# A fused two-block transformer on one core: the gated branches' sum is kept by VectorE instead of GpSimd

## The chip, the core and the metric

The kernel runs on one core of a Trainium2 chip. The core has five engines, each with an instruction queue of its own that it works off in order: TensorE (PE in the profile, its weight loads PEld), VectorE (DVE), ScalarE (ACT), GpSimd (POOL) and SyncE (SP), which here issues the DMA transfers. The metric is the time of one execution on the device in microseconds (us).

## What is computed

Two blocks of two layers each, on 512 tokens of width 1024, in float32. The first block has a recurrent mixer and a sparse-attention mixer, each with a convolutional feed-forward part. The second block, in which the change lies, has in each layer a mixer of four branches, an expert layer and a gated embedding. The mixer, cut to what matters:

```python
h = rms_norm(x, g_mix[i])
o_a = gqa_block_attention(q, k, v)             # branch 0
o_b = bidir_ssd(z, xs, b, c, dt_f, dt_b, ...)  # branch 1
o_c = diff_block_attention(q1, q2, k1, k2, v, lam, rel_bias)   # branch 2, then a norm
o_d = spatial_gating(uv, ...)                  # branch 3
branches = jnp.stack([o_a, o_b, o_c, o_d], axis=2)
gates = jax.nn.sigmoid(h @ w_branch_gate[i]).reshape(b, s, 4, 1024)
merged = jnp.sum(gates * jnp.einsum('bsnc,ncd->bsnd', branches, w_branch[i]), axis=2)
x = x + merged @ w_out[i]
```

## The kernel before, in words

Activations lie with the channels on the 128 partitions: a tile of 128x512 holds 128 channels of all tokens, and eight of them are the whole width (index d or k). A float32 matrix product is made of three float32r products of a high and a low part (lines 439 to 441): the weights come as a stream of 512 KB chunks (wraw), ScalarE copies each to the high part wh (line 237) and VectorE subtracts it to get the low part wl (line 238). This happens for every chunk, all through the kernel.

The mixer computes the branches in the order 3 (spatial gating), 0 (grouped attention), 1 (SSD, a state-space scan in chunks), 2 (differential attention). While a branch runs, the gate and output products of the branch before it are laid between its steps: `fill` takes a step of the generator `gate_merge` after each step of the branch. For each of the eight d, `gate_merge` does this: eight matmul triples give the gate pg; VectorE scales it with the row norm RB (line 1201), ScalarE takes a tanh (line 1202), two triples give the branch's output pb. For the first branch VectorE writes (1 + tanh) * pb to the running sum m (line 1207). For the other three it writes the product to a buffer mu (line 1210), and GpSimd adds mu to m (line 1211). That is 3 x 8 adds per layer, 48 in all. The merge of branch 0 runs beside SSD, that of branch 1 beside differential attention, that of branch 2 at the end, when no branch is left.

After the last merge, `mixer_out` takes m: ScalarE makes the scaled high part xh (line 1259), VectorE the low part xl (line 1260), and TensorE multiplies with w_out. In the same place small loads are brought in: tri into the buffer RB once the last scaled gate has read it (line 2085), from which ScalarE makes cum (line 2086), and pt (line 2080), from which ph is made (line 348). SyncE also loads the experts' weights ahead there (line 1327).

The PSUM buffers of pg and pb come from a pool of three (mm). mg and mu share three buffers.

The names that the steps below need in the SSD branch: delta and dA come from a softplus, a chain of some twenty small VectorE operations (lines 576 to 586, dA in line 1560); conv scales a projection into pad (line 1595), starts a four-tap convolution on ScalarE (line 1597), adds the other taps on VectorE into cv (line 1599), takes a tanh (line 1602) and multiplies (line 1604 to xs, line 1606 to cv); bch and bcl are the high and low part of two such results (lines 348, 349), which lines 1636 to 1638 multiply; M are the decay products (line 1676).

The program is written in the order above, but the order of each engine's queue is made by a scheduler when the program is built, which goes by its own estimate of what each instruction costs. So a change of one instruction's engine can reorder all queues around it.

Of the kernel before, what the change touches and what calls it, by code (L numbers as in the profile page):

```python
# [202 lines left out]
def halves(t):  # L203
    return t.rearrange("p (a b) -> p a b", a=2)


def unwoven(t):
    return t.rearrange("p (b a) -> p a b", a=2)
# [74 lines left out]
class Kern:  # L283
# [904 lines left out]
    def gate_merge(self, l, n, o, tp, first):  # L1188
        nc = self.nc
        for d in range(KD):  # L1190
            key = ("w_branch_gate_2", l, n * D + d * P)
            if key in self.early:
                pg = self.early.pop(key)
            else:
                pg = self.psum()
                specs = [("w_branch_gate_2", l, k * P, n * D + d * P) for k in range(KD)]
                self.dense(pg, specs, self.xh, self.xl, part=(0, 4))
                yield
                self.dense(pg, specs, self.xh, self.xl, part=(4, KD))
            t = tp.tile([P, S], F32, name="mg", bufs=3)  # L1200
            nc.vector.tensor_mul(halves(t), unwoven(pg), halves(self.RB))
            nc.scalar.activation(t, t, AF.Tanh, scale=0.5)
            pb = self.psum()
            self.dense(pb, [("w_branch_2", (l, n), k * P, d * P) for k in range(2)], *o)
            m = self.mg[d // 4][:, d % 4]
            if first:
                nc.vector.scalar_tensor_tensor(halves(m), halves(t), 1.0, unwoven(pb), op0=OP.add, op1=OP.mult)
            else:
                u = tp.tile([P, S], F32, name="mu", tag="mg", bufs=3)
                nc.vector.scalar_tensor_tensor(halves(u), halves(t), 1.0, unwoven(pb), op0=OP.add, op1=OP.mult)  # L1210
                nc.gpsimd.tensor_add(m, m, u)  # L1211
            yield

    def weave(self, a, b, na, nb):
# [961 lines left out]
```

## Time and profile before

| what | us |
|---|---|
| median of 3 runs | 3472.54 |
| lowest and highest of the runs | 3471.07, 3486.43 |
| the profiled execution | 3472.88 |
| its span, first to last instruction | 3471.1 |
| TensorE busy in the span | 3351.6 |
| VectorE busy | 1708.6 |
| ScalarE busy | 1259.8 |
| GpSimd busy | 420.6 |
| the 48 adds of line 1211 on GpSimd | 70.6 |

The views come from one execution, recorded by the hardware's profiler; times inside it are counted from the span's start. The mixer of layer 0 lies at about 1360 to 1820 us, that of layer 1 at 2410 to 2870. A busy time is the time in which an engine had an instruction in flight; the ends of matmuls are modelled, so a share near 100% for TensorE means that its instructions follow each other without a visible gap. A wait is put down to the instruction that released it last.

### The profile page before, as it was taken

What the parts mean: (1) busy time and instruction counts of PE and PEld (TensorE: products, weight loads), DVE (VectorE), ACT (ScalarE), POOL (GpSimd) and SP (SyncE); (2) the same over time, 40 slices, a digit from 0 to 9 for tenths busy, and PEclk for the clock granted to TensorE, in tenths of its full rate; (3) what the DMA queues carried; (4) which work ended last, traced back from release to release, by engine and by line L of the source; (5) the groups of instructions that cost most, each with busy time, mean ns of one, the idle gap of its engine ahead of it and who ended that gap; (6) DMA issues with size and microseconds to landing.
All of it is one profiled execution on the core that took longest, in us unless ns stands there. A gap on an engine that the chain in (4) does not pass through costs nothing.

```text
span 3471.1 us, 42234 instructions
## 1 busy us (share of the span) xinstructions
PE 3351.6 (97%) x16172; PEld 2340.8 (67%) x16172; DVE 1708.6 (49%) x3191; ACT 1259.8 (36%) x2221; POOL 420.6 (12%) x334
## 2 busy tenths in 40 slices
PE   7899999999999999999999999999999999999997
PEld 6788888866588888876887433327876887433325
DVE  7755454477765454776664111016676664111015
ACT  6533233366543234435633100004435644100004
POOL 1111011022021011210012000002210012000002
PEclk9999999999999999999999999999999999999999
DMA  3233333301023323222255999994221255999993
GB/s 126 92 103 129 103 103 108 110 32 37 19 91 103 101 99 114 74 73 67 88 205 210 381 412 419 419 419 144 76 72 62 88 194 198 382 412 419 419 419 124
DMA packets 173491, 629.06 MB, mean 181 GB/s; under 512 B 19557, under 2 KB 20069, under 8 KB 172521
## 3 DMA queue, kind: packets, MB, share of 16 engines
q1 hardware_dynamic: 173288, 626.36, 48.3%
q8 instruction: 127, 2.08, 0.2%
q14 instruction: 76, 0.61, 0.1%
HBM read 618.14 MB, written 8.14 MB: 180 GB/s over the span
## 4 chain that ended last, share of the span: by engine, by line
PE 78%; DVE 10%; DMA 6%; ACT 3%; issue 1%; POOL 1%; DVEq 0%; SPq 0%; ACTq 0%; POOLq 0%
PE mm L439 14%; PE mm L440 14%; PE mm L441 14%; PE mm L1977 10%; PE o L1977 5%; DMA eraw<-in_exw 3%; DVE wl L238 2%; PE o L891 2%; PE t L875 1%; DMA wraw<-in_exw 1%; ACT wh L237 1%; PE mm L1959 1%; PE o L1647 1%; PE o L1786 1%; DMA raw<-in_exw 1%
## 5 line engine op out<-in xcount | busy, mean ns | idle before, releaser
L439 PE MATMUL mm<-xh,wh 128*128 128x512 f32 (+1 forms) x1936 | 750.7, 388 | 11.7 <-DVE mu L1210 5.5
L441 PE MATMUL mm<-xh,wl 128*128 128x512 f32 (+1 forms) x1936 | 744.0, 384 | 2.7 <-DVE wl L238 2.7
L440 PE MATMUL mm<-xl,wh 128*128 128x512 f32 (+1 forms) x1936 | 743.6, 384 | 0.0
L238 DVE TENSOR_TENSOR wl<-wraw,wh 128x1024 fp32r<-128x1024 f32 x366 | 458.2, 1253 | 353.3 <-ACT wh L237 344.1
L237 ACT ACTIVATE wh<-wraw 128x1024 fp32r<-128x1024 f32 x378 | 398.3, 1055 | 521.9 <-PE mm L440 365.1
L439 PEld LDWEIGHTS mm<-xh,wh 128*128 128x128 f32 (+1 forms) x1936 | 368.5, 190 | 79.6 <-issue 9.0
L441 PEld LDWEIGHTS mm<-xh,wl 128*128 128x128 f32 (+1 forms) x1936 | 367.7, 190 | 63.6 <-issue 5.8
L440 PEld LDWEIGHTS mm<-xl,wh 128*128 128x128 f32 (+1 forms) x1936 | 368.6, 190 | 60.1 <-issue 8.2
L1977 PE MATMUL mm<-eraw,xe 128*64 128x512 f32 x1024 | 241.9, 597 | 1.0 <-DMA eraw<-in_exw 1.0
L371 POOL TENSOR_TENSOR sq<-sq,sqt 128x512 f32<-128x512 f32 x63 | 88.3, 1401 | 1240.8 <-ACT sqt L368 1233.6
L1983 DVE TENSOR_TENSOR hid<-sg,mm 128x512 f32<-128x512 f32 x32 | 22.0, 688 | 364.8 <-PE mm L1977 364.8
L1977 PE MATMUL mm<-raw,xe 128*64 128x512 f32 x656 | 161.9, 599 | 1.3 <-DMA raw<-in_exw 1.1
L1977 PEld LDWEIGHTS mm<-eraw,xe 128*64 128x64 f32 x1024 | 70.6, 136 | 134.6 <-issue 116.1
L612 POOL TENSOR_TENSOR fc<-fc,RB 128x512 f32<-128x512 f32 x48 | 84.8, 1766 | 546.7 <-ACT fc L611 546.7
L439 PE MATMUL mm<-gh,wh 128*128 128x512 f32 x384 | 145.5, 379 | 0.0
L440 PE MATMUL mm<-gl,wh 128*128 128x512 f32 x384 | 145.5, 379 | 0.0
L441 PE MATMUL mm<-gh,wl 128*128 128x512 f32 x384 | 145.5, 379 | 0.0
L1977 PE MATMUL o<-eraw,hidT 128*64 128x512 f32 x560 | 137.2, 605 | 3.9 <-DMA eraw<-in_exw 3.0
L1211 POOL TENSOR_TENSOR mg<-mg,mu 128x512 f32<-128x512 f32 x48 | 70.6, 1470 | 556.1 <-DVE mu L1210 510.8
L2031 ACT ACTIVATE yh<-o,af 128x512 fp32r<-128x512 f32 x32 | 22.0, 687 | 299.0 <-PE o L1977 299.0
L1982 ACT ACTIVATE sg<-mm 128x512 f32<-128x512 f32 x32 | 19.1, 597 | 288.8 <-PE mm L1977 288.6
L2032 DVE SCALAR_TENSOR_TENSOR yl<-o,af,yh 128x512 fp32r<-128x512 f32 x32 | 24.0, 751 | 202.9 <-ACT yh L2031 202.8
(522 smaller groups left out, 5623.6 us busy)
## 6 DMA issues: line engine op xcount, KB each, us to landing
eraw<-in_exw SPq DMA_DIRECT2D x396, 512.0 KB, 9.9
wraw<-in_wst SPq DMA_DIRECT2D x378, 512.0 KB, 3.3
raw<-in_exw SPq DMA_DIRECT2D x234, 512.0 KB, 9.9
wraw<-in_exw SPq DMA_DIRECT2D x136, 512.0 KB, 9.9
pbd<-pbs SPq DMA_DIRECT2D x8, 512.0 KB, 4.8
pb<-pbd SPq DMA_DIRECT2D x4, 1024.0 KB, 11.7
tb<-t5d SPq DMA_DIRECT2D x8, 448.0 KB, 3.2
mixt<-in_mix SPq DMA_DIRECT2D x2, 1344.0 KB, 6.4
```

The lines of the kernel that those rows point to most:

```text
L237: kb.nc.scalar.activation(h, raw, AF.Copy)
L238: (kb.nc.gpsimd if self.pool else kb.nc.vector).tensor_sub(l, raw, h.bitcast(F32))
L371: nc.gpsimd.tensor_add(acc, acc, t)
L439: nc.tensor.matmul(out, a, h, start=(k == 0), stop=False)
L440: nc.tensor.matmul(out, a, l, start=False, stop=False)
L441: nc.tensor.matmul(out, b, h, start=False, stop=(k == n - 1))
L612: nc.gpsimd.tensor_mul(c0, c0, self.RB)
L875: nc.tensor.transpose(pt[:, r * P:(r + 1) * P], srcs(i, r), self.ident)
L891: nc.tensor.matmul(o[0][c % 2 * HD:(c % 2 + 1) * HD], lhs(i), pe, start=(c < 2), stop=False)
L1211: nc.gpsimd.tensor_add(m, m, u)
L1647: nc.tensor.matmul(py[hh * HD:(hh + 1) * HD, sl], xd[:, i, q, h * HD:(h + 1) * HD], MS[hh][:, sl], start=(q == 0 and i == 0), stop=(q == 1 ...
L1977: nc.tensor.matmul(ps[e * CAP:(e + 1) * CAP], x[:, k, off + e * CAP:off + (e + 1) * CAP], raw[:, e], start=(k == 0), stop=(k == KD - 1))
```

## The change

Line 1211, the add of mu to the running sum m, is given to VectorE. Nothing else in the source changes, and the same values are computed.

```diff
             else:
                 u = tp.tile([P, S], F32, name="mu", tag="mg", bufs=3)
                 nc.vector.scalar_tensor_tensor(halves(u), halves(t), 1.0, unwoven(pb), op0=OP.add, op1=OP.mult)
-                nc.gpsimd.tensor_add(m, m, u)
+                nc.vector.tensor_add(m, m, u)
             yield
```

The built program differs in all queues from the start of the SSD branch to the output projection, in both layers alike, and nowhere else. On GpSimd the 24 adds per layer are gone and the rest stands as before. On TensorE the same matmuls stand in another order: between line 1552 and line 1562 there are 58 matmuls of projections where there were 42, and of the gate that follows the conv part 1 stands ahead of line 1636 and 2 ahead of line 1637, where 8 and 12 stood. On SyncE some weight loads (line 226) have moved ahead of an expert load (line 1327) or of pt.

VectorE at the start of the SSD branch, in the softplus (names sp_), a piece of the difference:

```order
 L576 TENSOR_SCALAR sp_u<-sp_e 128x32
 L585 TENSOR_SCALAR sp_r<-dx 128x32
-L1201 TENSOR_TENSOR mg<-mm,RB 128x512
+L1211 TENSOR_TENSOR mg<-mg,mu 128x512
 L577 RECIPROCAL sp_u<-sp_u 128x32
+L1201 TENSOR_TENSOR mg<-mm,RB 128x512
+L578 TENSOR_TENSOR sp_z<-sp_e,sp_u 128x32
 L1593 MEMSET pad 128x2
 L1594 MEMSET pad 128x2
-L578 TENSOR_TENSOR sp_z<-sp_e,sp_u 128x32
 L579 TENSOR_TENSOR sp_z_12230<-sp_z 128x32
-L1210 SCALAR_TENSOR_TENSOR mu<-mg,mm 128x512
```

The first add now stands where the next scaled gate stood, and that has moved behind the reciprocal. The second add follows four rows further down, and a second weight split, a fourth step of line 1599 and a second pad (line 1595) now stand ahead of line 1560.

VectorE at the end of the conv part, up to the second bcl, before:

```order
L1201 TENSOR_TENSOR mg<-mm,RB 128x512
L1606 SCALAR_TENSOR_TENSOR cv<-th,cv 128x512
L1594 MEMSET pad 128x2
L1210 SCALAR_TENSOR_TENSOR mu<-mg,mm 128x512
L238 TENSOR_TENSOR wl<-wraw,wh 128x1024
L349 TENSOR_TENSOR bcl_12540<-cv,bch_12539 128x512
```

and now:

```order
L1211 TENSOR_TENSOR mg<-mg,mu 128x512
L1599 SCALAR_TENSOR_TENSOR cv<-pad,cw,cv 128x512
L238 TENSOR_TENSOR wl<-wraw,wh 128x1024
L1606 SCALAR_TENSOR_TENSOR cv<-th,cv 128x512
L1201 TENSOR_TENSOR mg<-mm,RB 128x512
L1593 MEMSET pad 128x2
L349 TENSOR_TENSOR bcl_12540<-cv,bch_12539 128x512
```

The scaled gate and mu stood ahead of the split and of bcl. Now the split comes first, mu comes after bcl, and an add stands ahead of the last step of line 1599.

ScalarE at the tail, around the last xh, before:

```order
L1202 ACTIVATE mg<-mg 128x512
L237 ACTIVATE wh<-wraw 128x1024
L1259 ACTIVATE xh<-mg 128x512
L2086 ACTIVATE cum<-RB 128x128
L348 ACTIVATE ph<-pt 128x1024
L237 ACTIVATE wh<-wraw 128x1024
```

and now:

```order
L1202 ACTIVATE mg<-mg 128x512
L237 ACTIVATE wh<-wraw 128x1024
L2086 ACTIVATE cum<-RB 128x128
L1259 ACTIVATE xh<-mg 128x512
L237 ACTIVATE wh<-wraw 128x1024
L348 ACTIVATE ph<-pt 128x1024
```

The copy cum has passed the last xh, and the next wh has passed ph. On VectorE, in the same place, the last add stands behind mu and the weight split that follows it.

## Rows read from the trace of the kernel before

**Rows 1.** The page's first part: busy us, share of the span, instructions.

```profile
PE 3351.6 (97%) x16172; PEld 2340.8 (67%) x16172; DVE 1708.6 (49%) x3191; ACT 1259.8 (36%) x2221; POOL 420.6 (12%) x334
```

**Rows 2.** Busy windows, layer 0's mixer: us, PE, PEld, DVE, ACT, POOL, clock, DMA.

```profile
1508.00:1558.00 50.00, 46.38 (x220) 38.22 (x218) 43.59 (x99) 19.46 (x28) 6.67 (x4) 1.00 0.26 85
1558.00:1640.00 82.00, 81.40 (x343) 53.71 (x343) 53.81 (x85) 44.45 (x110) 5.60 (x4) 1.00 0.18 58
...
1678.00:1757.00 79.00, 78.06 (x467) 66.31 (x466) 69.74 (x195) 54.07 (x134) 9.85 (x7) 1.00 0.21 66
...
sum 312.00, PE 303.55 PEld 243.61 DVE 217.82 ACT 154.04 POOL 35.49; mean PE 60.71 PEld 48.72 DVE 43.56 ACT 30.81 POOL 7.10
```

**Rows 3.** Waits of PE, whole run: us in total, times, longest.

```profile
PE mm L439 <- DVE mu L1210: 5.5, 4, 2.4
...
PE t L1562 <- DVE dA L1560: 3.4, 2, 1.7
...
PE s L1637 <- DVE bcl L349: 2.5, 4, 0.7
PE s L1636 <- ACT bch L348: 2.3, 2, 1.2
```

**Rows 4.** Line L1211: ns min/median/max, and one of its waiters.

```profile
L1211 POOL TENSOR_TENSOR mg<-mg,mu x48: 1265/1280/2851, 1511.5 to 2863.6; 128x512 f32<-128x512 f32 x48
...
  ACT xh L1259: 4.8, 2
```

**Rows 5.** Timeline of DVE, end of the conv part: start, us, instruction, idle before.

```profile
1544.23 0.68 DVE L349 TENSOR_TENSOR bcl<-cv,bch 128x512 fp32r<-128x512 f32 x1
1544.83 0.74 DVE L1599 SCALAR_TENSOR_TENSOR cv<-pad,cw,cv 128x512 f32<-128x512 f32 x1
...
1546.75 1.21 DVE L238 TENSOR_TENSOR wl<-wraw,wh 128x1024 fp32r<-128x1024 f32 x1
1547.88 1.76 DVE L1599 SCALAR_TENSOR_TENSOR cv<-pad,cw,cv 128x512 f32<-128x512 f32 x1
...
1552.10 2.17 DVE L238 TENSOR_TENSOR wl<-wraw,wh 128x1024 fp32r<-128x1024 f32 x1 [0.26 <-ACT wh L237]
1554.19 0.68 DVE L349 TENSOR_TENSOR bcl<-cv,bch 128x512 fp32r<-128x512 f32 x1
```

**Rows 6.** One GpSimd add, DVE beside it, and line L1676 of layer 0.

```profile
1513.71 1.27 POOL L1211 TENSOR_TENSOR mg<-mg,mu 128x512 f32<-128x512 f32 x1 [0.95 <-DVE mu L1210]
...
1513.77 1.26 DVE L583 TENSOR_SCALAR sp_s<-sp_s 128x32 f32<-128x32 f32 x1
1515.06 0.19 DVE L582 TENSOR_TENSOR sp_s<-sp_s,sp_z 128x32 f32<-128x32 f32 x1
1515.29 0.18 DVE L583 TENSOR_SCALAR sp_s<-sp_s 128x32 f32<-128x32 f32 x1
...
L1676 DVE TENSOR_TENSOR M<-M,G x32: 278/545/1390, 1560.7 to 1629.7; 128x512 f32<-128x512 f32 x8, 128x384 f32<-128x384 f32 x8, 128x256 f32<-128x256 f32 x8, 128x128 f32<-128x128 f32 x8
```

**Rows 7.** Timeline of PE, first and last of 23 matmuls in a row.

```profile
1807.66 0.38 PE L440 MATMUL mm<-xl,wh 128*128 128x512 f32 x1
...
1812.41 0.38 PE L441 MATMUL mm<-oh,wl 128*128 128x512 f32 x1
```

**Rows 8.** The tail: DVE, PE, then the tri load's landing time.

```profile
1807.66 1.53 DVE L1260 SCALAR_TENSOR_TENSOR xl<-mg,xh 128x512 fp32r<-128x512 f32 x1 [0.46 <-ACT xh L1259]
...
1812.66 0.68 DVE L1201 TENSOR_TENSOR mg<-mm,RB 128x512 f32<-128x512 f32 x1
...
1815.19 0.48 PE L439 MATMUL mm<-xh,wh 128*128 128x512 f32 x1 [2.40 <-DVE mu L1210]
...
DMA to landing us min/median/max: 3.5/3.5/3.5
```

**Rows 9.** Windows after dA's wait and after the tail's gap (clock third from last).

```profile
1524.00:1528.00 4.00, 4.00 (x24) 3.35 (x23) 3.77 (x13) 2.29 (x4) 0.00 (x0) 1.00 0.41 131
...
1816.00:1820.00 4.00, 4.00 (x13) 3.20 (x11) 0.96 (x2) 0.83 (x2) 1.39 (x1) 0.57 0.67 227
```

## The prediction

> **What bounds the kernel now.** I read the page's busy shares first [rows 1]: TensorE is busy 97% of the span, VectorE 49%, GpSimd 12%. A share of the whole span says nothing about the stage that the change touches, so I then cut the mixer of layer 0 into its branches [rows 2]. In 312 us TensorE is busy 303.6 us there: 8.4 us are idle. Layer 1 repeats the pattern, so 17 us is all that taking waits away in the mixers could give, apart from what the clock gives back. VectorE is the engine nearest to its limit: 43.6 of 50 us at the start of the SSD branch, 69.7 of 79 us in the differential branch.
>
> The waits of TensorE over the whole run [rows 3] say which instruction ends each idle stretch; these come once or twice per layer. Per layer: 1.7 us for dA (the softplus chain on VectorE), 1.16 us for bch (ScalarE, behind VectorE's cv), 0.72 us for the first bcl and 0.51 for the second, and 2.4 us for the last mu, which holds the PSUM buffer that the output projection takes. All but bch name VectorE. None names GpSimd: the 48 adds (median 1.28 us, up to 2.85) [rows 4] are waited for by the scaled copy xh alone, 4.8 us in all, while ScalarE has slack.
>
> **What an add costs and frees.** A 128x512 float32 SBUF operation of the same kind lasts 0.68 us on VectorE, and the next starts 0.60 us after it started [rows 5]. The change puts 48 x 0.60 = 28.8 us onto VectorE, 14.4 per layer, and takes 70.6 us off GpSimd, which nothing needs.
>
> It also frees something. While a GpSimd add runs, some VectorE instructions last until it ends: a softplus step of 0.18 us took 1.26, and ended 0.05 us after the add that had started just before it; a cv step took 1.76 for 0.74, a weight split 2.17 for 1.21, an xl of the tail 1.53 for 0.68 [rows 5, 6, 8]. These come to 1.08 + 1.02 + 0.96 + 0.85 = 3.9 us. About ten more in layer 0, three M products among them (longest 1.39, median 0.55 us) [rows 6], are 0.1 to 1.1 us too long; I put them at 6 us together. So 14.4 us go on and some 10 come off: VectorE's load grows by about 4.4 us in 312.
>
> The Trainium skill (SBUF — State Buffer, "SBUF: two separate sides") says that GpSimd, and VectorE in some of its modes or with two SBUF inputs, take a shared port pair as an exclusive lock for a whole instruction. The stretched softplus step agrees. If every add shut VectorE out for its whole 1.28 us, 24 x 1.28 = 30.7 us would come off, and VectorE's load would fall by 16 us per layer; the rows show a third of it, since many VectorE instructions beside an add keep their time, so I keep 10.
>
> **The change, place by place (per layer).** Every order from SSD to the output projection is rearranged by the scheduler, so I take each of TensorE's waits by itself.
>
> *dA, 1.68 us.* Ahead of dA VectorE now has two adds (1.20) and, moved forward, one weight split (1.14), one cv step (0.67), one pad (0.60) and one xs (0.60): 4.2 us, less the 1.08 of the stretched step, 3.1 us. TensorE has 58 projection matmuls ahead of that point where it had 42; at (1812.41 - 1807.66)/22 = 0.216 us each [rows 7] that is 3.45 us. The wait would be 1.68 + 3.1 - 3.45 = 1.3 us. The softplus steps follow one another at 0.23 us though they last 0.18 or 0.19 [rows 6]: something put between them costs less than its length, up to 0.1 us at each of seven new places. That leaves 0.6. I take a gain of 0.7 (0.4 to 1.1).
>
> *bch and bcl, 1.88 us.* From the end of the last cv step of this pair, 1549.64, to the end of its second bcl, 1554.87, VectorE had L1201, L1606, mu, a stretched split and bcl: 5.2 us [rows 5]. Now it has split, L1606, L1201, bcl: 1.14 + 0.60 + 0.60 + 0.68 = 3.0, and the add ahead of them (0.60) costs less than the stretch that goes (1.02). So bcl comes 2.6 us sooner, and bch, which has also passed a weight copy on ScalarE, about 1.0 us. TensorE asks sooner too: of the following gate's matmuls 1 and 2 stand ahead of the two products, where 8 and 12 stood, 1.5 and 2.2 us. Alone this gives a wait of 1.7 us for bch and none for bcl. VectorE has 6.4 us idle in this stretch [rows 2], part of it between the conv steps, and any of it that its new order fills pulls bch forward. Gain 0.7 (0 to 1.9).
>
> *SSD states.* Four adds (2.4 us) against stretched M products and a split (about 2.5); VectorE has 28 of 82 us free [rows 2]. Zero, also for the second bcl's 0.51.
>
> *Differential branch.* Eight adds, 4.8 us, against some 1.3 us of stretched ones (part of the 6): 3.5 us more in a stretch where VectorE has 9.3 us free [rows 2]. TensorE is idle only 0.9 us there, with its weights for the merge as cover. If that cover is gone, each add sits ahead of a row maximum or a copy that TensorE's next transposes want, 3.5 us at most. I take a loss of 0.5, nearer to the end without, because VectorE at 90% has been keeping up (0 to 3.5).
>
> *Tail, 2.40 us.* Before: the add of d = 6 stretched the first xl to 1.53 us, the split and four xl followed, and L1201 of d = 7 started at 1812.66; TensorE restarted at 1815.19 when mu was done [rows 8]. Now the add (0.60) stands ahead of the first xl, mostly in the 0.46 us in which VectorE had waited, the xl lasts 0.68, and the split behind it can start some 0.5 us sooner. All that follows is bound by VectorE, so mu and the restart move by 0.5 (0 to 0.9). The last add now stands behind mu and a split (1.13), so it ends near 1816.4. Its xh stands behind cum, which waits for the tri load; that load starts when L1201 lets RB go and lands 3.5 us later [rows 8], near 1816.4. TensorE needs this xh 21 matmuls (4.5 us) after its restart, at 1819: hidden, unless the load takes 2.7 us longer. On SP the pt load is passed by one 512 KB weight load; ph is needed only at the end of the output projection.
>
> **Sum.** 0.7 + 0.7 + 0.5 - 0.5 = 1.4 us per layer, 2.8 in all. The expert layer runs close to the DMA's limit, but its loads are freed by TensorE's reads, so an earlier start passes through. The span 3471.1 becomes 3468.3; the profiled execution (3472.88) 3470.1; set against the median, 3472.54, it is **3469.7 us**, 0.1% less. About 0.5% (17 us) is what a measurement of this kernel can tell from no change.
>
> **Rivals.**
> *Slower: the differential branch's queue.* All 3.5 us per layer reach TensorE, and the first two terms come out at their lower ends (0.4 and 0): 2 x (3.5 - 0.4 - 0.5) = +5.2, 3477.7 us. For it: 90% busy, results wanted at once. Against: TensorE's 0.9 us of idle in the stretch. It decides once new waits there pass 1.9 us per layer, the other three terms.
> *Faster: the clock after the tail's gap.* After the gap of 2.40 us the granted clock is 0.57 from 1816 to 1820, much of it at the lower level; after dA's wait of 1.68 us it stays 1.00 [rows 9]. The new gap, 1.9 us, lies between. If it escapes the drop, 4 us of work at 0.57 would take 2.3: 1.7 us per layer, 3.4 in all, 3466.3. It is nearer to the gap that cost nothing, but no row settles it.
> *Slower by far: every add exposed.* 48 x 0.60 = +28.8, 3501 us. This needs VectorE to be the limit everywhere in the mixers; the 94 us of 312 in which it is idle in layer 0 [rows 2] speak against it. The Trainium skill (Perfetto Trace Analysis, "Identifying the Most-Contended Engine") judges engines by occupancy, which speaks against moving work from an engine at 12% to one at 49%; the rows say that neither share bounds the stage.
>
> **How the numbers follow.** Forecast 0.58; differential queue 0.20; clock 0.16; all exposed 0.03; something unseen in the new orders 0.03. The bounds of the terms give 2 x (1.1 + 1.9 + 0.9 + 1.7) = 11.2 us below the median and 2 x (3.5 - 0.4) = 6.2 above, 3461.3 to 3478.7; the range is 3461 to 3480. Faster by over 0.5% has 0.02, slower by over 0.5% 0.04, within it 0.94.
>
> **What would show it.** dA's wait near 1.0 us, bch and bcl together near 1.2, the tail's gap near 1.9; no VectorE softplus step above 0.3 us; TensorE's idle per mixer near 7 us. New waits of TensorE for row maxima, e or pe between SSD and tail would prove the slower rival; a clock of 1.00 after the tail's gap the faster one. Changes outside the mixers would make the argument wrong.

## The result, and the profile after

The changed kernel takes 3450.91 us (median of 11 runs, 3447.37 to 3470.46), the kernel before 3472.54. The ratio of the two is 0.9931, with a 95% interval of 0.9911 to 0.9951: the change makes the kernel 0.7% faster. The prediction, 3469.7 us within 3461 to 3480, missed it by 19 us.

Single executions of one kernel lie up to 25 us apart, mostly because TensorE stands at its lower clock for 17 to 75 us of the first 1470 us, ahead of everything that the change touches; the sections below therefore compare stretches of the mixers, which at the same clock repeat to 0.04 us (one exception: the differential branch before, 143.90 us in layer 0 and 144.24 in layer 1). The first row is the changed kernel, the second the experiment e9, whose first 1480 us are built alike. Columns of every windows view here: the stretch, its length, busy us (and number of instructions) of PE, PEld, DVE, ACT and POOL, the granted clock, the DMA share and GB/s.

```profile
7.44:1471.01 1463.57, 1425.70 (x6840) 1175.25 (x6840) 878.72 (x1604) 657.09 (x1078) 239.03 (x186) 0.99 0.27 90
```

```profile
7.10:1486.87 1479.77, 1442.70 (x6839) 1191.36 (x6840) 878.19 (x1604) 657.21 (x1078) 239.32 (x186) 0.98 0.27 89
```

The page's first part of the changed kernel, against [rows 1]:

```profile
span 3445.6 us, 42169 instructions
...
PE 3335.4 (97%) x16172; PEld 2336.3 (68%) x16172; DVE 1714.5 (50%) x3239; ACT 1260.9 (37%) x2221; POOL 349.7 (10%) x286
```

The span is 25.5 us shorter. GpSimd lost its 71 us. VectorE took 48 adds of 0.687 us, each of which puts off the next instruction by some 0.60 us ([rows 5]), 28.8 us in all, but is only 5.9 us busier, so about 23 us of stretched time went away. TensorE does the same 16172 matmuls in 16.2 us less busy time: 8.5 us of it stand in the two mixers at full clock, most of the rest is time at the lower clock. A reader who looks at waits alone does not find these 8.5 us.

The waits of TensorE in the changed kernel, against [rows 3] (us in total, times, longest), and the line of the adds, against [rows 4] (ns min/median/max):

```profile
PE mm L439 <- DVE mu L1210: 4.5, 4, 1.9
...
PE t L1562 <- DVE dA L1560: 1.1, 2, 0.5
...
PE s L1636 <- ACT bch L348: 0.2, 1, 0.2
```

```profile
L1211 DVE TENSOR_TENSOR mg<-mg,mu x48: 680/686/693, 1506.5 to 2838.6; 128x512 f32<-128x512 f32 x48
```

The waits for dA, bch and bcl fall from 8.2 to 1.3 us, and mu's by 1.0: together 7.9 us for both layers, a third of what the span lost.

Now the mixer of layer 1, in three stretches that begin and end at the same matmuls in every kernel (records 12036, 12550, 13364 and 13576 of TensorE's 16172): the SSD branch, the differential branch, and the tail into the output projection. Before:

```profile
2558.00:2681.11 123.11, 118.87 (x516) 84.34 (x514) 92.91 (x173) 60.57 (x133) 12.28 (x8) 1.00 0.21 70
2681.11:2825.35 144.24, 142.24 (x816) 122.84 (x816) 100.16 (x253) 76.64 (x168) 14.30 (x10) 1.00 0.32 109
2825.35:2875.45 50.10, 47.71 (x214) 41.17 (x213) 28.00 (x32) 19.06 (x27) 8.50 (x7) 0.97 0.71 252
```

After:

```profile
2541.27:2658.23 116.96, 116.15 (x515) 84.33 (x514) 90.73 (x181) 60.88 (x133) 0.00 (x0) 1.00 0.21 73
2658.23:2799.96 141.73, 140.60 (x815) 123.03 (x814) 103.47 (x264) 77.05 (x168) 0.00 (x0) 1.00 0.32 108
2799.96:2849.59 49.63, 47.71 (x214) 41.13 (x213) 30.21 (x38) 18.90 (x27) 0.00 (x0) 0.97 0.75 260
```

The SSD branch lost 6.15 us, the differential branch 2.51, the tail 0.47: 9.1 us in layer 1 (8.8 in layer 0), 18 in both. (In layer 0 the tail lost 1.7 us more, by the clock.) The expert layer in between neither gives nor takes: from the end of layer 0's mixer to layer 1's SSD branch the lead of the changed kernel grows by 1.2 us, about as much as its shorter time at the lower clock explains. The rest of the 25.5 us stands at the start, where the two executions differ by their clock.

VectorE's instructions beside the adds, in the SSD branch of layer 1, before (us busy, mean ns, then the idle time ahead):

```profile
L1599 DVE SCALAR_TENSOR_TENSOR cv<-pad,cw,cv 128x512 f32<-128x512 f32 x24 | 19.0, 790 | 1.2 <-ACT cv L1597 0.9
L1676 DVE TENSOR_TENSOR M<-M,G 128x512 f32<-128x512 f32 (+3 forms) x32 | 15.9, 540 | 1.0 <-ACT M L1674 0.8
```

and after:

```profile
L1599 DVE SCALAR_TENSOR_TENSOR cv<-pad,cw,cv 128x512 f32<-128x512 f32 x24 | 17.9, 747 | 1.1 <-ACT cv L1597 0.9
L1676 DVE TENSOR_TENSOR M<-M,G 128x512 f32<-128x512 f32 (+3 forms) x32 | 14.6, 486 | 2.1 <-ACT M L1674 1.8
```

The same instructions are shorter without GpSimd beside them. Three things could then have made the gain: GpSimd out of VectorE's way, the new order of the queues, and, against both, the adds on VectorE. The experiments take them apart.

### The profile page after: what moved, and what is told of

It reads as the page before. It is cut to its first block, busy times and chain, and to the rows that moved or that the text cites. A ratio compares the mean times of both kernels' runs of the same rounds, so it can differ in the third digit from the quotient of the medians.

```text
span 3445.6 us, 42169 instructions
## 1 busy us (share of the span) xinstructions
PE 3335.4 (97%) x16172; PEld 2336.3 (68%) x16172; DVE 1714.5 (50%) x3239; ACT 1260.9 (37%) x2221; POOL 349.7 (10%) x286
## 4 chain that ended last, share of the span: by engine, by line
PE 78%; DVE 10%; DMA 6%; ACT 3%; issue 1%; POOL 1%; DVEq 0%; SPq 0%; ACTq 0%; POOLq 0%
PE mm L439 14%; PE mm L440 14%; PE mm L441 14%; PE mm L1977 12%; PE o L1977 4%; DMA eraw<-in_exw 3%; DVE wl L238 2%; PE o L891 2%; DMA raw<-in_exw 1%; PE t L875 1%; PE mm L1959 1%; PE o L1786 1%; DMA wraw<-in_exw 1%; PE o L1647 1%; PE t L1529 1%
## 5 line engine op out<-in xcount | busy, mean ns | idle before, releaser
L1977 PEld LDWEIGHTS mm<-eraw,xe 128*64 128x64 f32 x1024 | 70.7, 136 | 133.9 <-issue 116.5
L1977 PEld LDWEIGHTS mm<-raw,xe 128*64 128x64 f32 x656 | 44.7, 136 | 87.5 <-issue 62.0
```

The lines of the kernel that those rows point to most:

```text
L1977: nc.tensor.matmul(ps[e * CAP:(e + 1) * CAP], x[:, k, off + e * CAP:off + (e + 1) * CAP], raw[:, e], start=(k == 0), stop=(k == KD - 1))
```

## Experiments: order against engine

The scheduler lays out each engine's queue when the program is built. TensorE's order comes out the same whether the adds are on GpSimd or left out; it changes only when they load VectorE. To part the order from the engine, a helper ties each instruction of TensorE, VectorE, ScalarE and SyncE to the one that it is to follow, by an order edge that adds no semaphore; the list is taken from the other build.

```diff
             kb.build(only2)
+            keep_order(tc, nc, ORDERS)
```

**e1: adds on GpSimd, the order of the changed kernel.**

> The 48 adds stay on GpSimd, as before, but TensorE, VectorE, ScalarE and SyncE are held to the order of instructions that the changed kernel has (before 3472.5 us, after 3450.9). Theory O (the gain comes with the new order of the queues): about 3453 us. Theory L (the gain comes from taking GpSimd's adds away from beside VectorE's work): about 3468 us, of which only the few short matmuls that now stand together, some 2 us per layer, are gained. If both count: between, near 3460.

Measured: 3457.36 us, ratio to before 0.9952 (0.9925 to 0.9980), nearest to the reading by which both count. SSD and differential branch of layer 1:

```profile
2560.86:2679.09 118.23, 116.34 (x516) 84.53 (x514) 90.48 (x173) 60.85 (x133) 11.16 (x8) 1.00 0.22 72
2679.09:2821.21 142.12, 140.63 (x815) 123.18 (x814) 101.19 (x254) 77.08 (x168) 13.72 (x10) 1.00 0.31 108
```

Not one add has moved, and 7.0 of the 9.1 us per layer are there (4.88 and 2.12). VectorE's instructions are as stretched as before: line 1599 takes 786 ns, line 1676 542.

**e2: adds on VectorE, the order of the kernel before.** The line of the change and the helper together.

> The adds are on VectorE as in the changed kernel, but TensorE, VectorE, ScalarE and SyncE are held to the order of the kernel before, the adds put in where they fit. Theory O: about 3471 us, or slower, since VectorE carries 29 us more in a queue not laid out for it. Theory L: about 3455 us, since GpSimd no longer stretches VectorE's instructions; the conv adds of line 1599 then take about 746 ns as in the changed kernel, not 790.

Measured: 3471.29 us, ratio 1.0001 (0.9978 to 1.0024). The two branches, and the largest wait of TensorE in the differential one:

```profile
2557.07:2678.47 121.40, 118.72 (x516) 84.34 (x514) 92.27 (x181) 60.57 (x133) 0.00 (x0) 1.00 0.21 71
2678.47:2826.21 147.74, 142.47 (x816) 122.72 (x816) 102.70 (x263) 77.21 (x168) 0.00 (x0) 1.00 0.31 106
```

```profile
PE t L1529 <- DVE e L1779: 3.1, 2, 1.8
```

The change of engine alone gives nothing on the whole. The SSD branch is 1.7 us shorter, the differential branch 3.5 us longer than before, and TensorE waits there for e: this is the prediction's slower rival, at its price. Line 1599 takes 748 ns, as expected. The adds stand where they fitted into VectorE's old queue; other places for them in it were not tried.

**e5 and e6: no adds at all.** The line is left out, in the old order (e5) and in the new one (e6).

```diff
-                nc.vector.tensor_add(m, m, u)
+                pass
```

> The 48 adds are left out (the three branches after the first then don't reach the sum), and every queue is held to the order of the kernel before. So neither GpSimd nor VectorE does this work. If the adds' own work beside VectorE were what costs (theory L), this is the most that can be had: about 3450 us or less, as the changed kernel. If the order decides (theory O), the old order keeps most of its length without any add: about 3466 us, that is 3 us less per layer than before, and the 16 dense matmuls that stand behind the dA matmul instead of ahead of it keep the first stretch of the SSD branch (where 104 matmuls took 22.83 us before, 21.79 in the changed kernel) over 22.3 us.

> The 48 adds are left out, and every queue is held to the order of the changed kernel. Theory O: 3447 to 3451 us, hardly under the changed kernel, since in this order VectorE has room for the adds; all that the 29 us of adds on VectorE still cost is the difference, at most 2 us per layer. Theory L: the same time as with the adds left out in the old order.

Measured: e5 3455.43 us, ratio 0.9953 (0.9928 to 0.9978); e6 3449.61 us, ratio 0.9930 (0.9907 to 0.9952). Neither theory had e5: it lies between the two. e6 lies where theory O had it. The rows of e5, then of e6:

```profile
2543.94:2663.01 119.07, 118.28 (x516) 84.23 (x514) 87.79 (x173) 60.71 (x133) 0.00 (x0) 1.00 0.22 73
2663.01:2806.49 143.48, 141.96 (x815) 123.01 (x815) 97.05 (x253) 76.53 (x168) 0.00 (x0) 1.00 0.32 109
2806.49:2854.43 47.94, 46.02 (x213) 39.99 (x212) 26.16 (x32) 19.02 (x27) 0.00 (x0) 1.00 0.73 259
```

```profile
2539.62:2655.89 116.27, 115.64 (x515) 84.38 (x514) 86.44 (x173) 60.93 (x133) 0.00 (x0) 1.00 0.22 73
2655.89:2797.49 141.60, 140.43 (x815) 123.34 (x814) 97.94 (x254) 76.99 (x168) 0.00 (x0) 1.00 0.31 109
```

With these the six cases stand side by side (layer 1, us; the tail at full clock: before as e1 shows it, after as its own layer 0 does):

| adds | order | SSD | differential | tail |
|---|---|---|---|---|
| GpSimd | old (before) | 123.11 | 144.24 | 48.4 |
| GpSimd | new (e1) | 118.23 | 142.12 | 48.42 |
| none | old (e5) | 119.07 | 143.48 | 47.94 |
| none | new (e6) | 116.27 | 141.60 | 47.94 |
| VectorE | old (e2) | 121.40 | 147.74 | 47.94 |
| VectorE | new (after) | 116.96 | 141.73 | 47.94 |

Along the way before, e5, e6, after, a layer loses 4.04 + 0.76 + 0.5 = 5.3 us when GpSimd is out of the way, 2.80 + 1.88 = 4.7 by the order, and gets 0.69 + 0.13 = 0.8 back for the adds on VectorE. In the old order the same adds on VectorE cost 2.33 + 4.26 = 6.6, more than GpSimd's. The shares hang on the way taken: along before, e1, e6, after, the order comes first and is worth 7.0 us, and taking the adds off GpSimd is then worth only 1.96 + 0.52 + 0.48 = 3.0. So the gain is neither the engine's nor the order's alone: of the two orders VectorE takes the adds almost for nothing only in the one that was laid out for them.

**e3: GpSimd's work once more, with nobody waiting for it.** The changed kernel, its order held, with a copy of each add on GpSimd.

```diff
-                nc.vector.tensor_add(m, m, u)
+                nc.vector.tensor_add(m, m, u); nc.gpsimd.tensor_add(self.scr, m, m)
...
-            tp = es.enter_context(self.tc.tile_pool(name="mtmp", bufs=2))
+            tp = es.enter_context(self.tc.tile_pool(name="mtmp", bufs=2)); self.scr = tp.tile([P, S], F32, name="scr", bufs=1)
```

> The changed kernel with its order held, and behind each add on VectorE one more add of the same size on GpSimd that writes a scratch tile and that nothing waits for. It prices GpSimd's work beside VectorE by itself. Theory L: VectorE's line 1599 back to about 790 ns and the time back to about 3465 us or more. Theory O: no more than 2 us over the changed kernel, 3451 to 3453.

Measured: 3473.84 us, ratio 1.0010 (0.9989 to 1.0031). SSD and differential branch of layer 1, and two waits at its tail, of SyncE's queue and of TensorE:

```profile
2569.44:2690.47 121.03, 118.37 (x516) 85.82 (x515) 94.31 (x181) 60.72 (x133) 12.08 (x8) 0.99 0.21 70
2690.47:2833.38 142.91, 141.10 (x816) 122.95 (x814) 106.04 (x264) 76.80 (x168) 11.26 (x10) 1.00 0.31 108
```

```profile
SPq L1327 <- POOL scr L1211: 2.7, 1, 2.7
```

```profile
PE mm L439 <- ACT wh L237: 4.6, 1, 4.6
```

Against the changed kernel the SSD branch is 4.07 us longer (of which 1.7 are 3.4 us at the lower clock) and the differential branch 1.18: 3.5 us per layer for work that nothing reads, since VectorE is 6.2 us busier beside it. Line 1599, of which the expectation speaks, is not what suffers: it stays at 746 ns, while line 238 goes from 1220 to 1273 and line 1676 from 486 to 512. TensorE's wait for dA is back at 1.5 us. The time of the whole overstates the price. At the tail an expert load waits for the scratch tile's memory, a weight load stands behind it in SyncE's queue, and TensorE waits 4.6 us for that weight: an accident of this experiment.

**e4: only the adds beside the differential branch.**

```diff
-                nc.gpsimd.tensor_add(m, m, u)
+                (nc.vector if n == 1 else nc.gpsimd).tensor_add(m, m, u)
```

> Only the 16 adds of branch 1, which stand beside the differential branch, are on VectorE; the 32 others stay on GpSimd. The stretch beside the differential branch became 2.4 us shorter per layer in the changed kernel: by that, if each stretch gains by itself, 3472.5 - 4.8 = about 3468 us, with the stretch of the SSD branch as before. If instead the gain of a stretch hangs on what is moved in the other, the differential branch keeps its old length.

Measured: 3464.08 us, ratio 0.9982 (0.9957 to 1.0007). The branches:

```profile
2550.12:2673.24 123.12, 118.89 (x515) 84.41 (x514) 92.91 (x173) 60.58 (x133) 12.28 (x8) 1.00 0.21 70
2673.24:2815.01 141.77, 140.70 (x816) 123.27 (x815) 101.24 (x261) 77.09 (x168) 2.56 (x2) 1.00 0.31 108
```

SSD as before, the differential branch as after: the gain of the differential branch does not hang on what is moved in the SSD branch. (The other way round was not run.)

## Experiments: what in the order

The order is worth 2.80 us in the SSD branch even without any add, and the waits in the profile hardly say so: 2.64 of it is TensorE's busy time (118.28 to 115.64, e5 to e6). One thing that differs is the number of places where TensorE's dense matmuls (lines 439 to 441) meet the short ones of line 1647: by the built order 38 such places per layer before, 30 after. The timeline of PE in the changed kernel shows what such a place costs:

```profile
2587.63 1.07 PE L1647 MATMUL o<-M,xd 128*64 128x512 f32 x2
2588.64 0.48 PE L439 MATMUL mm<-xh,wh 128*128 128x512 f32 x1
2589.05 1.07 PE L1647 MATMUL o<-M,xd 128*64 128x512 f32 x2
2590.05 0.48 PE L440 MATMUL mm<-xl,wh 128*128 128x512 f32 x1
...
2590.90 0.86 PE L1647 MATMUL o<-M,xd 128*64 128x384 f32 x2
2591.69 0.48 PE L440 MATMUL mm<-xl,wh 128*128 128x512 f32 x1
2592.10 0.86 PE L1647 MATMUL o<-M,xd 128*64 128x384 f32 x2
```

Each short matmul makes 64 columns of output, for one of two heads, and shows as two records. Split up by dense matmuls, the four matmuls (eight records) take 1.07 + 1.07 + 0.86 + 0.86 = 3.86 us.

**e9: the changed kernel with the short matmuls brought together.** Its order is held, but in 14 spots over both layers up to three dense matmuls that stood between two runs of short ones now come ahead of both, which takes away 13 meeting places per layer. In TensorE's order, schematically:

```diff
-L1647  L439  L1647
+L439  L1647  L1647
```

> The changed kernel, all queues held to its order but for one thing: in 14 places over the two layers where up to three dense matmuls stand between two runs of the SSD branch's short matmuls (line 1647), the dense ones now come first and the short ones stand together; 26 fewer changes from one kind to the other. In the changed kernel's trace a short one behind a dense one starts 309 ns after it and a dense one behind a short one 202 to 522 ns after it, where dense ones follow each other at 216. If the changes themselves cost (theory O, by the form of the order): 13 per layer at 0.1 to 0.2 us, so the stretch of the SSD branch's states (272 matmuls, 61.41 us) falls to 59 to 60 us in both layers, 3447 to 3449 us in all. If they only stand where TensorE would wait for VectorE's product of M anyway: 61.4 us or more, and no change in all.

Measured: 3447.0 us, ratio 0.9916 (0.9886 to 0.9946). The SSD branch of layer 1; the same eight records in the timeline; and a narrow window on the timeline that holds the first two matmuls, one of each head:

```profile
2553.33:2665.58 112.25, 111.44 (x515) 84.28 (x514) 90.76 (x181) 60.76 (x133) 0.00 (x0) 1.00 0.23 76
```

```profile
2600.78 1.90 PE L1647 MATMUL o<-M,xd 128*64 128x512 f32 x8
```

```profile
2600.78 1.08 PE L1647 MATMUL o<-M,xd 128*64 128x512 f32 x4
```

The eight records take 1.90 us in place of 3.86. Two short matmuls that follow each other directly run side by side: in the trace the two heads' matmuls start 7 ns apart, and both, four records, are done in 1.08 us, where one alone took 1.07. The Trainium skill (TensorE: Matmul & The Clock Gate, "Part 3: Packing small matmuls — row/col tiling") says that small matmuls in different tiles of the array run at the same time; this trace agrees, and the changed kernel's shows that one dense matmul between them ends it. The branch falls by 4.71 us, all of it busy time of TensorE (116.15 to 111.44), 0.36 for each meeting place that is gone: the 272 matmuls of the expectation take 59.03 us, and the stretch ahead of them, where the first of the short ones stand, gives as much again. The two layers give 9.4 us. The medians are only 4 us apart, because half of e9's executions have a mean clock of 0.983 or 0.984; the three at 0.990 take 3437.3 to 3439.6 us, against 3447.4 to 3451.8 for the eight of the changed kernel at 0.989 or 0.990.

**e11: the same in the kernel before,** adds on GpSimd, old order; 22 spots, 20 meeting places less per layer.

> The kernel before, its adds on GpSimd and every queue in its own order, but for the SSD branch's short matmuls (line 1647), which are brought together in 22 places over the two layers, as in the grouped run of the changed kernel. Theory P (two of these matmuls, which write 64 columns each, run side by side when nothing stands between them, 7 ns apart in place of 100 to 480): some 12 pairs more per layer at about 0.38 us, so the stretch of 401 matmuls that holds them (98.1 us in layer 1 before) falls to 93 to 95 us without any add being moved, and the whole to 3462 to 3465 us. Rival: with GpSimd's adds beside it VectorE delivers the products M no earlier, TensorE waits for them instead, and the stretch stays over 97 us.

Measured: 3458.16 us, ratio 0.9956 (0.9931 to 0.9981). The SSD branch of layer 1:

```profile
2548.34:2666.54 118.20, 113.96 (x515) 85.57 (x513) 92.72 (x173) 60.49 (x133) 12.27 (x8) 0.99 0.22 72
```

It falls from 123.11 to 118.20, or to 116.5 without the 3.4 us at the lower clock: 6.6 us, 0.33 for each place. The 401 matmuls of the expectation, which the lower clock does not touch, fall from 98.09 to 91.53 us, more than the 3 to 5 us expected. The two prices give 8 x 0.33 to 8 x 0.36 = 2.6 to 2.9 us for the 8 places that the change took away. The order was worth 2.80 us in this branch, 2.4 of it in the part where the short matmuls stand. What the order does for the differential branch (1.88 us) was not taken apart and stays open: the number of places where dense matmuls (there lines 439 to 441 and 1175 to 1177) give way to others is nearly the same (52 before, 53 after), so this price does not explain it.

**e7 and e8: further work from GpSimd to VectorE,** each on the changed kernel: the scaling of e (e7), the sums of squares (e8).

```diff
-            nc.gpsimd.tensor_scalar(e, e, den, 1.0, op0=OP.mult, op1=OP.mult)
+            nc.vector.tensor_scalar(e, e, den, 1.0, op0=OP.mult, op1=OP.mult)
```

```diff
-        nc.gpsimd.tensor_add(acc, acc, t)
+        nc.vector.tensor_add(acc, acc, t)
...
-            self.nc.gpsimd.tensor_add(self.sq, self.sq, self.sqlast)
+            self.nc.vector.tensor_add(self.sq, self.sq, self.sqlast)
```

> The changed kernel with 32 more instructions taken from GpSimd to VectorE: the scaling of e by its denominator at line 1497 (851 ns each on GpSimd). TensorE waited for it 1.4 us in two waits, and its order of instructions hardly moves (44 of 13920 rows). If a move pays where the order stays: 1 to 3 us off, about 3449 us. If it pays only by the order that comes with it: within 1 us of 3451, in spite of 27 us of GpSimd work gone.

> The changed kernel with the adds of the squares (lines 371 and 425, 76 instructions, 1.4 us each on GpSimd, 108 us in all) on VectorE. TensorE's order moves in few places (86 of 13920 rows). TensorE waits 2.0 us in five waits for line 425 now; at 0.69 us on VectorE in place of 1.5 these waits would fall to nothing: 2 to 4 us off, about 3448 us. Against it: VectorE is the one that TensorE waits for at the ends of the stages, and 76 x 0.69 = 52 us more stand in its queue; then no gain, or up to 5 us lost.

Measured: e7 3452.68 us, ratio to before 0.9941 (0.9917 to 0.9966), no different from the changed kernel; e8 3434.81 us over four executions, ratio 0.9884 (0.9848 to 0.9919), 16 us under it and better than expected. In e8 both branches keep their length (116.98 and 141.71 us in layer 1); its gain lies outside the mixers. Matmul by matmul, with half of the time at the lower clock taken off, e8's profiled execution is some 10 us shorter than the changed kernel's, nearly all of it in three stretches: 3.4 between 882 and 1098 us, 2.9 between 2217 and 2446, 3.8 after 3149. The waits for line 425 were 2.0 us in all; why the stretches became that much shorter is not taken apart here.

**e10 and e12: both together,** the sums of squares on VectorE and the short matmuls grouped, e12 the same kernel as e10 in further executions.

> The kernel with the adds of the branches and the sums of squares on VectorE (3434.8 us), its order held but for the same 14 places. If the changes of kind cost: 3431 to 3433 us; if not: 3434 to 3436.

> The branch adds and the sums of squares on VectorE, with the short matmuls brought together: the version that the runs so far point to as the best. Its first measurement (3436.5 us) held only executions in which TensorE stood longer at its lower clock in the first 1469 us, a stretch in which nothing was changed. If that was chance: 3420 to 3428 us in the other executions, a ratio near 0.985 to the kernel before; if the version itself brings it on: 3436 us again.

Measured: e10 3436.45 us, ratio 0.9893 (0.9862 to 0.9923), all four of its executions at a mean clock of 0.985 to 0.986; e12 3421.21 us, ratio 0.9848 (0.9819 to 0.9877). By its time alone e10 bears out the reading by which the grouping gives nothing, 3434 to 3436. In e12 four of six executions have a mean clock of 0.991 or 0.992 and take 3420.4 to 3421.4 us, so the version itself does not bring the lower clock on; its SSD branch takes 112.24 us in layer 1, as in e9. Taken together the ten executions of this one kernel have a median of 3431.8 us, 19 us under the changed kernel and 41 under the one before; e12's median alone says 30 and 51. It is the fastest version that was run.

## Why the prediction was wrong, point by point

- **The adds' price and the relief.** Predicted per layer: 14.4 us on, about 10 off, 4.4 net. Summed over the three stretches of layer 1, VectorE's busy time rose from 92.91 + 100.16 + 28.00 = 221.1 us to 90.73 + 103.47 + 30.21 = 224.4, by 3.3, and fell to 87.79 + 97.05 + 26.16 = 211.0, by 10.1, when the adds were only taken from GpSimd (e5). Right to about 1 us. Had every add shut VectorE out for its whole length, which is the exclusive lock of the Trainium skill (SBUF — State Buffer, "SBUF: two separate sides") applied to every VectorE instruction, it would have been 30.7 us per layer; the measured 10.1 again is a third of it.
- **dA.** Predicted wait about 1.0 us (gain 0.7, 0.4 to 1.1); measured 0.54, a gain of 1.14. The direction and the reason were right, the size came out at the upper bound. The wait is 0.6 us in e5 (no adds, old order), 0.7 in e1 (GpSimd, new order) and still 1.7 in e2 (VectorE, old order): GpSimd out of the way is enough, or the new order, but not the new engine in the old order.
- **bch and bcl.** Predicted gain 0.7 (0 to 1.9); measured 1.7, inside the bounds, at the end that was not chosen.
- **SSD states: zero. This step failed.** It weighed VectorE's adds against VectorE's stretches and found them equal, as they nearly are; it took for granted that TensorE's time there depends on nothing else. The states alone lost 3.0 us per layer (272 matmuls, 64.40 to 61.41). GpSimd out of the way takes 0.9 of it (before to e5), the second bcl's wait of 0.51, which the step had kept, among it; the order takes 2.3 without any add (e5 to e6): the fewer places where dense and short matmuls meet. The diff of the order was at hand; its rows on TensorE were read for how much cover they give ahead of a wait, never for what stands next to what. The stretch before and after:

```profile
2616.70:2681.10 64.40, 63.80 (x273) 42.83 (x271) 44.48 (x66) 34.60 (x84) 5.59 (x4) 1.00 0.21 68
```

```profile
2596.80:2658.20 61.40, 61.28 (x273) 42.81 (x272) 42.74 (x68) 34.65 (x84) 0.00 (x0) 1.00 0.21 69
```

- **Differential branch: a loss of 0.5 (0 to 3.5). This step failed too.** It gained 2.5 us. The loss of 3.5 us is real, but only in the old order (e2); the new order turns it into a gain. The step priced the adds as if they were put into the queue that the profile shows, while the change also lays out that queue anew. What in the new order gives the gain is not shown.
- **Tail.** Predicted gap 1.9 us, gain 0.5; measured 1.91 in layer 0 (this row answers to the restart in [rows 8]) and a gain of 0.47. Right.

```profile
1801.33 0.48 PE L439 MATMUL mm<-xh,wh 128*128 128x512 f32 x1 [1.91 <-DVE mu L1210]
```

- **The bound of 17 us.** "All that taking waits away could give" was TensorE's idle time in [rows 2]. The mixers gave 18 us, of which 8.5 are busy time: in the SSD branch of one layer it fell by 118.87 - 116.15 = 2.7 us, with the same matmuls. Busy time is not a floor: matmuls that run side by side shorten it (e9). The range and the 0.02 for faster were added up from waits alone and were wrong with it.
- **The faster rival, the clock after the tail's gap.** The tail of the changed kernel, from the last projection of the gate on, layer 0 and layer 1:

```profile
1793.86:1811.58 17.72, 15.81 (x74) 13.53 (x72) 12.64 (x17) 10.05 (x16) 0.00 (x0) 1.00 0.68 240
2830.18:2849.59 19.41, 17.49 (x74) 14.67 (x73) 13.40 (x18) 10.01 (x16) 0.00 (x0) 0.91 0.66 221
```

  The price was right (1.7 us), the condition not: with the same gap of 1.9 us the drop is absent in one layer and present in the other, and in e1 the old gap of 2.4 us brings no drop in either layer:

```profile
1814.04:1832.24 18.20, 15.80 (x74) 13.54 (x72) 12.18 (x15) 10.09 (x16) 3.42 (x2) 1.00 0.67 226
2851.43:2869.63 18.20, 15.81 (x74) 13.55 (x72) 12.04 (x15) 9.87 (x16) 3.41 (x2) 1.00 0.65 219
```

  What decides it stays open. That layer 0 escaped the drop gave 1.7 us, by luck.
- **Every add exposed (3501 us).** Did not happen; even in the old order 6.6 of the 14.4 us per layer reached TensorE.
- **Expert layer unchanged.** Right: an earlier start passes through.
- **"None names GpSimd."** True of the five waits of the mixer, but not of the whole run that [rows 3] are taken from: TensorE waits there 3.3 us for line 425 and 1.4 for line 1497, both on GpSimd.

```profile
PE t L396 <- POOL sq L425: 3.3, 5, 1.6
PE t L1529 <- POOL e L1497: 1.4, 2, 0.7
```

Per layer the sum missed 0.4 us at dA, 1.0 at bch and bcl, 3.0 at the SSD states and 3.0 at the differential branch, 7.4 of the 7.7 us by which the predicted 1.4 fell short of 9.1.

## What to carry to other kernels

Where a scheduler lays out the queues, a one-line change of engine is two changes, and the second can be the larger: hold the old order with the new engine, and the new order with the old engine, before saying which of them pays. Read a diff of TensorE's order for neighbours, not only for cover: short matmuls that could run side by side are worth bringing together, and the profile calls the loss busy time, not waiting. And take the work of a slow engine off the side of a loaded one only with an eye on the queue that receives it: the same adds cost 0.8 us per layer in one order and 6.6 in another.

## What was not expected of the hardware

- Two matmuls of 64 output columns each take 1.08 us together when they follow each other directly, and 1.07 each when a dense matmul stands between them; grouping them gave 4.71 us per layer in the changed kernel and 6.6 in the one before, more than any wait of TensorE in the mixers.
- 24 GpSimd adds that TensorE never waits for cost it 5.3 us per layer in the old order (before against e5), 3.0 in the new one (e1 against e6), and some 3.5 as pure extra work there (e3); VectorE's instructions are stretched beside them, by 10.1 us per layer in the old order.
- The clock after a short gap is not set by the gap's length alone: 1.9 us brought a drop in one layer and none in the other (changed kernel), 2.4 us none in two (e1).
